# Global attention on one core: value products issued four key blocks at a time, score maxima from the full 128-row operand, and one product that places a chunk's maxima

## The chip, the cores and the metric

One core of a Trainium2 chip runs the whole program. The metric is device time in microseconds (us); the kernel before takes 3729.62 us, the median of 3 runs (3728.04 to 3729.76).

## What is computed

The reference is a one-layer encoder trunk over 2,048 + 256 tokens. Four mixers (neighbourhood attention, a state-space scan, global attention, a gated recurrence) share one input projection; their normalized outputs go through one output product, then come cross-attention to a memory and a convolutional gated feed-forward part. The change touches the global attention alone:

```
def attend_block(qi):
    s = jnp.einsum('bqhgd,bkhd->bhgqk', qi, k).astype(jnp.float32) * scale
    p = jax.nn.softmax(s, axis=-1).astype(v.dtype)
    return jnp.einsum('bhgqk,bkhd->bqhgd', p, v)
```

There are 4 query heads and 2 key/value heads of 64 features, so two query heads share a key head. The 2,048 sample tokens attend to each other, and the 256 prompt tokens to each other.

## The kernel before, in words

`stage_gqa` is a generator. For each of the two key heads (kv) it goes through five chunks of queries: four of 512 queries against 2,048 keys, and one of 256 queries against 256 keys. Keys stand in blocks of 128.

**Operands.** A float32 number is kept as a high and a low part. `ks` holds the high part of the keys twice, in rows 0 to 63 and in rows 64 to 127. For each query head `qs` holds the high part of the queries in the upper 64 rows and the low part in the lower 64, and `qa` the high part and, in its lower 64 rows, minus the maximum of each query. `ka` has the low part of the keys, zeros, and a row of ones against that maximum. So a score block `ps` is two products of 512 columns (L1470, L1471), over all 128 rows, and has its maximum subtracted already.

**Maxima (`gqa_prep`, L1413).** For 128 queries and 512 keys two products `pm`, one for each head, give scores from high parts only (L1429). They take 64 rows each: head 0 the upper half of the array, head 1 the lower, from an operand `qm` with both heads above one another. VectorE reduces each to a maximum (L1432, L1438). Then for each head four products on 64 columns (L1447) write the maxima of four query blocks in rows, and ScalarE copies them negated into `qa` (L1449). `pm` and `pb` share two PSUM buffers. `gqa_prep` yields after each pair of `pm`, and the scores of the chunk before call it: `prep_step()` after each second score, and after the first too in every third key block. So the maxima of a chunk are found during the scores of the chunk before it; those of each kv's first chunk come ahead of its scores.

**Scores (`GqaUnit.scores`, L1463).** After the two products ScalarE takes the exponential into `pe` (L1473). `ps` has two PSUM buffers. GpSimd adds `pe` to the running sum of the chunk, or VectorE for head 0 in odd key blocks (L1481).

**Values (`GqaUnit.values`, L1485).** For one key block two products of plain float32 (L1498), one for each head, go to the upper and the lower 64 columns of the array. Each appears in the trace as two records. They are called when more than AHEAD = 2 key blocks are in flight, so after every key block.

**Order.** TensorE's and SyncE's instructions stand in the order in which Python issues them; the other engines' order is set by the scheduler. `weave` runs `stage_gqa` against a filler, in turn the rest of the input projection, the gate of the state-space mixer (L1244, L1258), neighbourhood attention (L547, L567, L580) and products with the memory (L1588). Each number that `stage_gqa` yields is owed to the filler, and each filler step pays some of it off: FILL = 260 after each score and ahead of each block's values, so 780 for a key block.

Of the kernel before, what the change touches and what calls it, by code (L numbers as in the profile page):

```python
# [13 lines left out]
F32 = mybir.dt.float32  # L14
F32R = mybir.dt.float32r
I32 = mybir.dt.int32
U32 = mybir.dt.uint32
AF = mybir.ActivationFunctionType
ALU = mybir.AluOpType
AX = mybir.AxisListType  # L20
# [3 lines left out]
P = 128  # L24
# [23 lines left out]
UP, DN = slice(0, 64), slice(64, 128)  # L48


def f32(ap):
    return ap.bitcast(F32)
# [91 lines left out]
def drain(g):  # L144
    for _ in g:
        pass
# [1144 lines left out]
def stage_gqa(k, ctx, side=None):  # L1291

    nc, tc = k.nc, k.tc
    pp = ctx.enter_context(tc.tile_pool(name="gq_p", bufs=1, side=side, reuse_waits="tile"))
    wp = ctx.enter_context(tc.tile_pool(name="gq_w", bufs=2, side=side, reuse_waits="tile"))
    sm = ctx.enter_context(tc.tile_pool(name="gq_s", bufs=2, side=side, reuse_waits="tile"))
    ps_m = ctx.enter_context(tc.tile_pool(name="gq_pm", bufs=GQ_M, space=PSUM, side=side))
    ps_s = ctx.enter_context(tc.tile_pool(name="gq_ps", bufs=GQ_S, space=PSUM, side=side))
    ps_o = ctx.enter_context(tc.tile_pool(name="gq_po", bufs=1, space=PSUM, side=side))
    pools = (pp, wp, sm, ps_m, ps_s, ps_o)  # L1300
    chunks = [(c, 512, 0, T_S) for c in range(0, T_S, 512)] + [(T_S, T_P, T_S, T_P)]

    def steps():
        keys = gqa_tiles(k, pp)
        todo = [(kv, ch) for kv in range(2) for ch in chunks]
        loaded = []

        def fetch():
            if todo:
                loaded.append(gqa_queries(k, *todo.pop(0), wp))  # L1310

        for kv in range(2):
            gqa_keys(k, kv, keys)
            if not loaded:
                fetch()
            yield GQ_START
            preps = itertools.chain.from_iterable(gqa_prep(k, keys, ch, loaded, fetch, pools) for ch in chunks)
            ready = []

            def prep_step():  # L1320
                if not ready:
                    x = next(preps, None)
                    if x:
                        ready.append(x)

            flight, late = [], []

            def values():
                u = flight.pop(0)
                u.values()  # L1330
                if late:
                    if next(late[0], late) is late:
                        late.pop(0)
                if u.done:
                    late.append(u.finish())

            for ch in chunks:
                while not ready:
                    prep_step()
                    yield GQ_PREP  # L1340
                unit = GqaUnit(k, kv, keys, ch, ready.pop(0), pools)
                for kb in range(unit.nkb):
                    for h in range(2):
                        unit.scores(kb, h)
                        if h or kb % 3 == 2:
                            prep_step()
                        yield FILL
                    flight.append(unit)
                    if len(flight) > AHEAD:
                        yield FILL  # L1350
                        values()
            while flight:
                yield FILL_END
                values()
            for g in late:
                drain(g)
                yield FILL_END

    return steps()


FILL = 260
FILL_END = 1000
GQ_START = 6000
GQ_PREP = 800
AHEAD = 2
GQ_M = 2
GQ_S = 2
RPM = 3
# [1 line left out]

def gqa_tiles(k, pp):

    nc = k.nc
    ks = pp.tile([P, T], F32R, name="gq_ks")
    ka = pp.tile([P, T], F32R, name="gq_ka")
    va = pp.tile([P, NB, 64], F32, name="gq_va")
    nc.gpsimd.memset(f32(ka)[DN, :], 0.0)
    nc.gpsimd.memset(f32(ka)[64:65, :], 1.0)
    one = pp.tile([P, 1], F32, name="gq_one")  # L1380
    nc.vector.memset(one, 1.0)
    return ks, ka, va, one


def gqa_keys(k, kv, keys):
    nc, s = k.nc, k.s
    ks, ka, va = keys[:3]
    hs = slice(64 * kv, 64 * kv + 64)
    for rows, src, dst in ((UP, "kh", ks), (DN, "kh", ks), (UP, "kl", ka)):
        nc.sync.dma_start(out=f32(dst)[rows, :], in_=s[src][0, hs, :])  # L1390
    nc.sync.dma_start(out=va, in_=s["vc"][:, hs].rearrange("(b p) c -> p b c", p=P))


def gqa_queries(k, kv, chunk, wp):


    nc, s = k.nc, k.s
    q0, nq = chunk[:2]
    qsl = slice(q0, q0 + nq)
    qm = wp.tile([P, 512], F32R, tag="qm", name="qm", bufs=2)  # L1400
    nc.sync.dma_start(out=f32(qm)[:, :nq], in_=s["qh"][kv, :, qsl])
    out = []
    for h in range(2):
        qs = wp.tile([P, 512], F32R, tag=f"qs{h}", name="qs", bufs=3)
        qa = wp.tile([P, 512], F32R, tag=f"qa{h}", name="qa", bufs=3)
        hs = slice(64 * h, 64 * h + 64)
        for rows, src, dst in ((UP, "qh", qs), (DN, "ql", qs), (UP, "qh", qa)):
            nc.sync.dma_start(out=f32(dst)[rows, :nq], in_=s[src][kv, hs, qsl])
        out.append((qs, qa))
    return qm, out  # L1410


def gqa_prep(k, keys, chunk, loaded, fetch, pools):  # L1413


    nc = k.nc
    pp, wp, sm, ps_m, ps_s, ps_o = pools
    q0, nq, k0, nk = chunk
    ks = keys[0]
    nqb = nq // P  # L1420
    half = min(512, nk)
    qm, out = loaded.pop(0)
    fetch()
    mxs = [sm.tile([P, 4, 4], F32, tag=f"mx{h}", name="mx") for h in range(2)]
    for qb in range(nqb):
        for i, kc in enumerate(range(k0, k0 + nk, half)):
            pms = [ps_m.tile([P, 512], F32, tag="m", name="pm") for h in range(2)]
            for hs, pm in zip((UP, DN), pms):
                nc.tensor.matmul(pm[:, :half], lhsT=qm[hs, qb * P:qb * P + P], rhs=ks[hs, kc:kc + half],  # L1429
                                 start=True, stop=True)  # L1430
            for mx, pm in zip(mxs, pms):
                nc.vector.tensor_reduce(out=mx[:, qb, i:i + 1], in_=pm[:, :half], axis=AX.X, op=ALU.max)  # L1432
            yield None
    ms = []
    for h, mx in enumerate(mxs):
        if nk > half:
            m1 = sm.tile([P, 4], F32, tag=f"m1{h}", name="m1")
            nc.vector.tensor_reduce(out=m1[:, :nqb], in_=mx[:, :nqb], axis=AX.X, op=ALU.max)  # L1438
        else:
            m1 = mx[:, :, 0]  # L1440
        ms.append(m1)
    yield None
    for m1, (qs, qa) in zip(ms, out):
        yield None
        pb = ps_m.tile([P, 4, P], F32, tag="m", name="pb")
        for qb in range(nqb):
            nc.tensor.matmul(pb[DN, qb, :], lhsT=m1[:, qb:qb + 1].to_broadcast([P, 64]), rhs=k.ident,  # L1447
                             start=True, stop=True)
        nc.scalar.activation(out=qa[DN, :nq], in_=pb.rearrange("p a b -> p (a b)")[DN, :nq], func=AF.Copy,  # L1449
                             scale=-1.0)  # L1450
    yield out


class GqaUnit:
# [8 lines left out]
    def scores(self, kb, h):  # L1463
        k, nc, nq = self.k, self.k.nc, self.nq
        pp, wp, sm, ps_m, ps_s, ps_o = self.pools
        ks, ka = self.keys[:2]
        qs, qa = self.prep[h]
        ksl = slice(self.k0 + kb * P, self.k0 + kb * P + P)
        ps = ps_s.tile([P, 512], F32, tag="s", name="ps")
        nc.tensor.matmul(ps[:, :nq], lhsT=ks[:, ksl], rhs=qs[:, :nq], start=True, stop=False)  # L1470
        nc.tensor.matmul(ps[:, :nq], lhsT=ka[:, ksl], rhs=qa[:, :nq], start=False, stop=True)  # L1471
        pe = wp.tile([P, 512], F32, tag="pe", name="pe", bufs=2 * AHEAD + 6)
        nc.scalar.activation(out=pe[:, :nq], in_=ps[:, :nq], func=AF.Exp)  # L1473
        eng = nc.vector if h == 0 and kb % 2 else nc.gpsimd
        if kb == 0:
            self.sums[h] = pe
        else:
            t = self.sums[h]
            if kb == 1:
                t = wp.tile([P, 512], F32, tag=f"sum{h}", name="sum")  # L1480
            eng.tensor_tensor(out=t[:, :nq], in0=self.sums[h][:, :nq], in1=pe[:, :nq], op=ALU.add)  # L1481
            self.sums[h] = t
        self.ahead.append(pe)
# [752 lines left out]
```

## Time and profile before

| what | value |
|---|---|
| median of 3 runs | 3729.62 us |
| the profiled execution's own time | 3726.75 us |
| its span on the core | 3724.7 us |
| mean granted TensorE clock | 0.981 |
| TensorE busy (matmul) in the span | 96% |
| VectorE, ScalarE, GpSimd busy | 49%, 34%, 35% |
| first `pm`, last global attention product | at 923.2 us and about 1521 us |

The page gives busy shares of the whole span, the chain of work that ended last and the costliest groups by source line. Views of one stretch (busy time by window, groups by line in a window, who waited for whom, instructions in order of time) tell more of a stage. In the view in order of time the first number is the start, the second the time that a group of equal instructions was busy. Matmuls overlap their neighbours, so the step from one start to the next, not the busy time, is what an instruction takes of TensorE.

### The profile page before, as it was taken

Reading aid. Unit: us, or ns where it says so; the run is one execution under the profiler, and the core shown is the slowest. Engines: PE = TensorE matmul, PEld = TensorE weight load, DVE = VectorE, ACT = ScalarE, POOL = GpSimd, SP = SyncE. Lnnn points to the kernel's source line nnn. Section 1 sums busy time; section 2 is a strip of 40 time slices with the busy share of each in tenths; the row PEclk is TensorE's granted clock in tenths of the full one; section 3 lists DMA queues with packets and bytes.
Section 4 is the critical chain, followed back from the end, with each engine's and each line's share of the span. In section 5 each row is a group of like instructions: output and inputs, shape, how many; then the busy total and the mean of one; then the engine's idle time right before and its main releaser. Section 6 shows DMA issues by size and latency. Waiting matters only on the chain.

```text
span 3724.7 us, 53214 instructions
## 1 busy us (share of the span) xinstructions
PE 3581.3 (96%) x20150; PEld 3084.8 (83%) x20150; DVE 1822.1 (49%) x4422; ACT 1275.4 (34%) x2632; POOL 1301.0 (35%) x1110
## 2 busy tenths in 40 slices
PE   7998999999899999999998999999999999999998
PEld 6998998898445555678887999988999998999997
DVE  5757777565653644355555333326333336333334
ACT  3321114453345445444444222224322224322222
POOL 3326435343345244200001433433423333433342
PEclk9999999999799999999998999999999999999999
DMA  6453443333141411312224212214211223211221
GB/s 209 165 190 110 164 151 105 108 125 83 44 122 45 118 38 27 129 52 75 74 74 154 74 52 68 74 62 134 87 52 57 68 75 101 87 57 52 63 80 51
DMA packets 212833, 340.37 MB, mean 91 GB/s; under 512 B 82913, under 2 KB 155105, under 8 KB 208353
## 3 DMA queue, kind: packets, MB, share of 16 engines
q1 hardware_dynamic: 212576, 336.97, 28.6%
q8 instruction: 159, 2.61, 0.3%
q14 instruction: 98, 0.79, 0.1%
HBM read 252.14 MB, written 84.77 MB: 90 GB/s over the span
## 4 chain that ended last, share of the span: by engine, by line
PE 83%; DVE 8%; DMA 3%; issue 2%; ACT 2%; POOL 1%; SPq 0%; ACTq 0%; DVEq 0%; POOLq 0%
PE pg L123 5%; PE pa L123 5%; PE pa L124 5%; PE pa L125 5%; PE pg L124 5%; PE pg L125 5%; PE pd L123 5%; PE pd L125 5%; PE pd L124 5%; PE po L1498 4%; PE mm L123 3%; PE mm L125 3%; PE mm L124 3%; PE ps L123 2%; PE pa L691 2%; PE ps L124 2%
## 5 line engine op out<-in xcount | busy, mean ns | idle before, releaser
L1968 DVE SCALAR_TENSOR_TENSOR gc<-pg,f_cw,gc 128x384 f32<-128x384 f32 (+4 forms) x308 | 166.5, 558 | 563.2 <-ACT gc L1958 559.4
L117 POOL TENSOR_TENSOR ul<-raw,uh 128x1024 fp32r<-128x1024 f32 x132 | 317.6, 2406 | 209.3 <-ACT uh L116 206.3
L123 PE MATMUL pg<-h,uh 128*128 128x386 f32 x1056 | 358.7, 340 | 0.9 <-DVE x L1809 0.9
L124 PE MATMUL pg<-h,uh 128*128 128x386 f32 x1056 | 357.6, 339 | 0.0
L125 PE MATMUL pg<-h,ul 128*128 128x386 f32 x1056 | 357.0, 338 | 0.0
L123 PE MATMUL pa<-h,uh 128*128 128x384 f32 x1056 | 356.9, 338 | 0.0
L124 PE MATMUL pa<-h,uh 128*128 128x384 f32 x1056 | 356.5, 338 | 0.0
L125 PE MATMUL pa<-h,ul 128*128 128x384 f32 x1056 | 356.3, 337 | 0.0
L1994 DVE TENSOR_TENSOR acc<-acc,pd 128x512 f32<-128x512 f32 x264 | 181.4, 687 | 312.9 <-PE pd L125 312.8
L123 PE MATMUL pd<-dh,uh 128*128 128x512 f32 x792 | 316.4, 399 | 8.1 <-DVE h L166 5.5
L1976 POOL TENSOR_TENSOR ul<-gc,uh 128x384 fp32r<-128x384 f32 x132 | 134.8, 1021 | 541.1 <-ACT uh L1975 541.1
L125 PE MATMUL pd<-dh,ul 128*128 128x512 f32 x792 | 313.8, 396 | 0.0
L124 PE MATMUL pd<-dl,uh 128*128 128x512 f32 x792 | 313.7, 396 | 0.0
L1481 POOL TENSOR_TENSOR sum<-sum,pe 128x512 f32<-128x512 f32 x168 | 214.2, 1284 | 194.6 <-ACT pe L1473 188.5
L117 POOL TENSOR_TENSOR dl<-raw,dh 128x1024 fp32r<-128x1024 f32 x66 | 158.8, 2406 | 265.1 <-ACT dh L116 265.1
L1958 ACT ACTIVATE gc<-pg,f_cw 128x384 f32<-128x384 f32 x132 | 87.2, 661 | 419.0 <-PE pg L125 415.8
L123 PE MATMUL mm<-wh,hhi 128*128 128x256 f32 x720 | 212.7, 295 | 4.6 <-DVE ut L363 4.0
L1473 ACT ACTIVATE pe<-ps 128x512 f32<-128x512 f32 (+1 forms) x264 | 151.0, 590 | 188.2 <-PE ps L1471 185.5
L123 PE MATMUL mm<-hhi,wh 128*128 128x384 f32 x576 | 208.0, 361 | 0.0
L1432 DVE TENSOR_REDUCE mx<-pm 128x1 f32<-128x512 f32 (+1 forms) x264 | 170.7, 678 | 72.0 <-PE pm L1429 70.9
L124 PE MATMUL mm<-wl,hhi 128*128 128x256 f32 x720 | 205.0, 285 | 0.0
L125 PE MATMUL mm<-wh,hlo 128*128 128x256 f32 x720 | 204.8, 284 | 0.0
(491 smaller groups left out, 8704.2 us busy)
## 6 DMA issues: line engine op xcount, KB each, us to landing
raw<-in_w_up SPq DMA_DIRECT2D x132, 512.0 KB
raw<-in_w_down SPq DMA_DIRECT2D x66, 512.0 KB
x<-in_x SPq DMA_DIRECT2D x36, 512.0 KB
hhi<-s_h SPq DMA_DIRECT2D x8, 1536.0 KB
hlo<-s_h SPq DMA_DIRECT2D x8, 1536.0 KB
raw<-in_w_in SPq DMA_DIRECT2D x22, 512.0 KB
s_h<-hhi SPq DMA_DIRECT2D x6, 1536.0 KB
s_h<-hlo SPq DMA_DIRECT2D x6, 1536.0 KB
```

Source lines behind the costliest of these rows:

```text
L117: (eng or nc.gpsimd).tensor_tensor(out=l, in0=raw, in1=f32(h), op=ALU.subtract)
L123: mm(out, lhsT=lh, rhs=rh, start=first, stop=False)
L124: mm(out, lhsT=lh, rhs=rl, start=False, stop=False)
L125: mm(out, lhsT=ll, rhs=rh, start=False, stop=last)
L1432: nc.vector.tensor_reduce(out=mx[:, qb, i:i + 1], in_=pm[:, :half], axis=AX.X, op=ALU.max)
L1473: nc.scalar.activation(out=pe[:, :nq], in_=ps[:, :nq], func=AF.Exp)
L1481: eng.tensor_tensor(out=t[:, :nq], in0=self.sums[h][:, :nq], in1=pe[:, :nq], op=ALU.add)
L1498: nc.tensor.matmul(po[hs, :nq], lhsT=va[:, vt, :], rhs=pe[:, :nq], start=kb == 0, stop=self.done)
L1958: nc.scalar.activation(out=gc, in_=pg[:, 1:TG + 1], func=AF.Identity, scale=cw[:, f, 1:2], bias=cw[:, f, 3:4])
L1968: V.scalar_tensor_tensor(out=gc[:, a:b], in0=pg[:, a + off:b + off], scalar=cw[:, f, tap:tap + 1], in1=gc[:, a:b], op0=ALU.mult, op1=ALU.add)
L1976: nc.gpsimd.tensor_tensor(out=ul[:, cs], in0=gc, in1=f32(uh)[:, cs], op=ALU.subtract)
L1994: V.tensor_tensor(out=acc[b][:, ns], in0=acc[b][:, ns], in1=pd, op=ALU.add)
```

## The change

Three things change. **Values** are issued for four key blocks at once, when six are in flight (AHEAD + BATCH); ahead of them there is no yield any more, and FILL is 340, so a key block now owes 680 to the filler. `pe` gets 13 buffers in place of 10. **Maxima** come from `qs` and `ks` over all 128 rows, so `qm` and its load go, and both products of a pair use the whole array. **Placing:** the maxima of a chunk are reduced into columns 64 to 67 of a 128x128 tile of zeros (two sets of two tiles), one product with the identity turns it, and VectorE multiplies its lower half, spread over the query blocks, by a small matrix `place` with -1 on its diagonal. Each query's row then has its maximum in one of four rows of `qa`, and `ka` has ones in these four.

```
             def values(n):
                 for _ in range(n):
                     u = flight.pop(0)
                     u.values()
                     if u.done:
                         late.append(u.finish())
                 for _ in range(2):
                     if late and next(late[0], late) is late:
                         late.pop(0)
...
                     flight.append(unit)
-                    if len(flight) > AHEAD:
-                        yield FILL
-                        values()
-            while flight:
-                yield FILL_END
-                values()
+                    if len(flight) == AHEAD + BATCH:
+                        values(BATCH)
+            yield FILL_END
+            values(len(flight))
...
-FILL = 260
-FILL_END = 1000
+FILL = 340
+FILL_END = 3000
 AHEAD = 2
+BATCH = 4
...
-    nc.gpsimd.memset(f32(ka)[64:65, :], 1.0)
+    nc.gpsimd.memset(f32(ka)[64:68, :], 1.0)
+    mzs = [[pp.tile([P, P], F32, name=f"gq_mz{i}{h}") for h in range(2)] for i in range(2)]
...
+    nc.vector.tensor_scalar(out=place[DN], in0=k.ident[DN, 64:68], scalar1=-1.0, scalar2=None, op0=ALU.mult)
...
-    qm = wp.tile([P, 512], F32R, tag="qm", name="qm", bufs=2)
-    nc.sync.dma_start(out=f32(qm)[:, :nq], in_=s["qh"][kv, :, qsl])
...
-            for hs, pm in zip((UP, DN), pms):
-                nc.tensor.matmul(pm[:, :half], lhsT=qm[hs, qb * P:qb * P + P], rhs=ks[hs, kc:kc + half],
+            for (qs, qa), pm in zip(out, pms):
+                nc.tensor.matmul(pm[:, :half], lhsT=qs[:, qb * P:qb * P + P], rhs=ks[:, kc:kc + half],
...
-        for qb in range(nqb):
-            nc.tensor.matmul(pb[DN, qb, :], lhsT=m1[:, qb:qb + 1].to_broadcast([P, 64]), rhs=k.ident,
-                             start=True, stop=True)
-        nc.scalar.activation(out=qa[DN, :nq], in_=pb.rearrange("p a b -> p (a b)")[DN, :nq], func=AF.Copy,
-                             scale=-1.0)
+        pb = ps_m.tile([P, P], F32, tag="m", name="pb")
+        nc.tensor.matmul(pb, lhsT=mz, rhs=k.ident, start=True, stop=True)
+        nc.vector.tensor_tensor(out=qa[DN, :nq].rearrange("p (b q) -> p b q", q=P),
+                                in0=pb[DN].unsqueeze(1).to_broadcast([64, nqb, P]),
+                                in1=place[DN, :nqb].unsqueeze(2).to_broadcast([64, nqb, P]), op=ALU.mult)
...
-        pe = wp.tile([P, 512], F32, tag="pe", name="pe", bufs=2 * AHEAD + 6)
+        pe = wp.tile([P, 512], F32, tag="pe", name="pe", bufs=2 * (AHEAD + BATCH) + 1)
```

The order of TensorE's instructions in the first chunk, before (`ps` scores or, on L1244, the filler's gate; `pm` maxima; `po` values):

```order
L1498 MATMUL po<-pe,gq_va 64x512 x2
L1470 MATMUL ps<-qs,gq_ks 128x512
L1471 MATMUL ps<-qa,gq_ka 128x512
L1244 MATMUL ps<-y_10162,gw 128x288
L1244 MATMUL ps<-y_10163,gw 128x288
L1244 MATMUL ps<-y_10162,gw 128x288
L1244 MATMUL ps<-y_10163,gw 128x288
L1470 MATMUL ps<-qs,gq_ks 128x512
L1471 MATMUL ps<-qa,gq_ka 128x512
L1429 MATMUL pm<-gq_ks,qm 128x512 x2
L1498 MATMUL po<-pe,gq_va 64x512 x2
```

And of the change, at the end of that chunk's scores (L1471 and L1472 are now the scores, L1499 the values, L1448 the product that places the maxima):

```order
L1244 MATMUL ps<-y_10168,gw 128x288
L1244 MATMUL ps<-y_10169,gw 128x288
L1244 MATMUL ps<-y_10168,gw 128x288
L1244 MATMUL ps<-y_10169,gw 128x288
L1471 MATMUL ps<-qs,gq_ks 128x512
L1472 MATMUL ps<-qa,gq_ka 128x512
L1499 MATMUL po<-pe,gq_va 64x512 x8
L1471 MATMUL ps<-qs,gq_ks 128x512
L1472 MATMUL ps<-qa,gq_ka 128x512
L1448 MATMUL pb<-ident,gq_mz_9930 128x128
L1471 MATMUL ps<-qs,gq_ks 128x512
L1472 MATMUL ps<-qa,gq_ka 128x512
```

Where one pair of value products followed each key block, eight now stand together. In the whole program there are 131 separate groups of value products before and 34 in the change, 72 products of maxima to rows before and 20 now; the 264 `pm`, 264 scores and 264 value products are all still there.

VectorE's order in the change, where the first chunk's maxima are placed (L1439 the reductions of `pm`, L1443 those into the tile of zeros, L1449 the multiplication into `qa`; L1233 to L1237 are the filler's):

```order
L1439 TENSOR_REDUCE mx<-pm 128x1 x2
L1237 SCALAR_TENSOR_TENSOR y_10168<-t,y_10168 128x576
L1233 TENSOR_SCALAR t<-t 128x576
L1443 TENSOR_REDUCE gq_mz_9928<-mx 128x4
L1443 TENSOR_REDUCE gq_mz_9929<-mx 128x4
L1235 TENSOR_TENSOR t<-t,y_10169 128x576
L1233 TENSOR_SCALAR t<-t 128x576
L1449 TENSOR_TENSOR qa<-pb,gq_place 64x512
L1237 SCALAR_TENSOR_TENSOR y_10169<-t,y_10169 128x576
L1449 TENSOR_TENSOR qa<-pb,gq_place 64x512
```

The write into `qa` has moved from ScalarE to VectorE, and stands there behind the filler's work.

## Rows read from the trace of the kernel before

**Rows 1.** The page: span, and busy time by engine.

```profile
span 3724.7 us, 53214 instructions
PE 3581.3 (96%) x20150; PEld 3084.8 (83%) x20150; DVE 1822.1 (49%) x4422; ACT 1275.4 (34%) x2632; POOL 1301.0 (35%) x1110
```

**Rows 2.** Busy us (instructions) by engine, granted clock, DMA share, GB/s, by window.

```profile
core 0: us, PE busy (x) PEld busy (x) DVE busy (x) ACT busy (x) POOL busy (x), PEclk, DMA share, GB/s
923.00:958.40 35.40, 28.77 (x114) 17.56 (x113) 28.28 (x48) 5.93 (x9) 4.64 (x3) 0.74 0.51 159
958.40:1046.50 88.10, 80.24 (x277) 37.02 (x276) 48.87 (x78) 39.99 (x69) 39.23 (x40) 0.87 0.06 19
1046.50:1106.70 60.20, 57.05 (x243) 27.74 (x241) 34.32 (x62) 29.46 (x54) 33.39 (x37) 1.00 0.41 133
1169.30:1212.20 42.90, 42.90 (x222) 24.77 (x220) 11.71 (x39) 24.40 (x59) 23.00 (x21) 1.00 0.17 45
```

**Rows 3.** TensorE in order of time, first chunk: start, us busy, instruction.

```profile
974.01 1.97 PE L1498 MATMUL po<-pe,gq_va 128*64 128x512 f32 x4
975.91 0.80 PE L1470 MATMUL ps<-qs,gq_ks 128*128 128x512 f32 x1
976.50 0.63 PE L1471 MATMUL ps<-qa,gq_ka 128*128 128x512 f32 x1
976.93 0.63 PE L1470 MATMUL ps<-qs,gq_ks 128*128 128x512 f32 x1
...
979.79 0.40 PE L1470 MATMUL ps<-qs,gq_ks 128*128 128x512 f32 x1
980.02 0.40 PE L1471 MATMUL ps<-qa,gq_ka 128*128 128x512 f32 x1
...
995.35 0.39 PE L1471 MATMUL ps<-qa,gq_ka 128*128 128x512 f32 x1
995.66 0.49 PE L1429 MATMUL pm<-gq_ks,qm 64*128 64x512 f32 x2
996.09 1.08 PE L1498 MATMUL po<-pe,gq_va 128*64 128x512 f32 x4
997.10 0.50 PE L1470 MATMUL ps<-qs,gq_ks 128*128 128x512 f32 x1
997.43 0.40 PE L1471 MATMUL ps<-qa,gq_ka 128*128 128x512 f32 x1
```

**Rows 4.** TensorE in order of time, the end of the second kv.

```profile
1515.49 1.08 PE L1498 MATMUL po<-pe,gq_va 128*64 128x256 f32 x8
1516.50 0.66 PE L1512 MATMUL pt<-ident,ou 128*128 128x128 f32 x4
```

**Rows 5.** TensorE in order of time, a placing of maxima.

```profile
1163.07 0.40 PE L1471 MATMUL ps<-qa,gq_ka 128*128 128x512 f32 x1
1163.39 0.65 PE L1447 MATMUL pb<-ident,mx 128*64 128x128 f32 x4
1163.98 0.55 PE L567 MATMUL pt<-ident,na_pe 128*128 128x128 f32 x3
```

**Rows 6.** VectorE's groups by line, 1046.5 to 1106.7 us: busy, mean ns, idle before.

```profile
L1432 DVE TENSOR_REDUCE mx<-pm 128x1 f32<-128x512 f32 x33 | 21.6, 685 | 7.9 <-PE pm L1429 7.7
L1481 DVE TENSOR_TENSOR sum<-sum,pe 128x512 f32<-128x512 f32 x7 | 4.8, 689 | 14.7 <-ACT pe L1473 14.7
```

**Rows 7.** ScalarE's exponentials, groups by line, 1169.3 to 1212.2 us.

```profile
L1473 ACT ACTIVATE pe<-ps 128x512 f32<-128x512 f32 (+1 forms) x26 | 13.9, 564 | 13.0 <-PE ps L1471 12.3 <-POOL sum L1481 0.6
```

**Rows 8.** TensorE's waits (us, times, longest), 1046.5 to 1106.7, then 958.4 to 974 us.

```profile
PE pm L1429 <- DVE mx L1432: 2.8, 4, 1.2
...
PE pm L1429 <- DVE mx L1432: 3.3, 2, 2.4
PE ps L1470 <- ACT pe L1473: 2.6, 2, 1.4
```

**Rows 9.** ScalarE's copies into `qa`: ns min/median/max, first and last start.

```profile
L1449 ACT ACTIVATE qa<-pb x20: 379/593/594, 956.8 to 1473.1; 64x512 fp32r<-64x512 f32 x16, 64x256 fp32r<-64x256 f32 x4
```

More of the change, by code (lines that the diff above doesn't have):

```diff
@@ L1326, in steps, with values @@
             flight, late = [], []
[L1328 to L1332, printed above, removed]
+            def values(n):
+                for _ in range(n):
+                    u = flight.pop(0)
+                    u.values()
+                    if u.done:
+                        late.append(u.finish())
+                for _ in range(2):
+                    if late and next(late[0], late) is late:
                         late.pop(0)
-                if u.done:
-                    late.append(u.finish())
             for ch in chunks:
@@ L1378, in gqa_tiles @@
     nc.gpsimd.memset(f32(ka)[DN, :], 0.0)
-    nc.gpsimd.memset(f32(ka)[64:65, :], 1.0)
+    nc.gpsimd.memset(f32(ka)[64:68, :], 1.0)
     one = pp.tile([P, 1], F32, name="gq_one")
     nc.vector.memset(one, 1.0)
-    return ks, ka, va, one
+    mzs = [[pp.tile([P, P], F32, name=f"gq_mz{i}{h}") for h in range(2)] for i in range(2)]
+    for mz in mzs:
+        for m in mz:
+            nc.gpsimd.memset(m, 0.0)
+    place = pp.tile([P, 4], F32, name="gq_place")
+    nc.vector.tensor_scalar(out=place[DN], in0=k.ident[DN, 64:68], scalar1=-1.0, scalar2=None, op0=ALU.mult)
+    return ks, ka, va, one, mzs, place
 def gqa_keys(k, kv, keys):
@@ L1409, in gqa_queries @@
         out.append((qs, qa))
-    return qm, out
+    return out
 def gqa_prep(k, keys, chunk, loaded, fetch, pools):
@@ L1418, in gqa_prep @@
     q0, nq, k0, nk = chunk
-    ks = keys[0]
+    ks, place = keys[0], keys[5]
     nqb = nq // P
     half = min(512, nk)
-    qm, out = loaded.pop(0)
+    out = loaded.pop(0)
     fetch()
+    mzs = keys[4][0]
+    keys[4].append(keys[4].pop(0))
     mxs = [sm.tile([P, 4, 4], F32, tag=f"mx{h}", name="mx") for h in range(2)]
@@ L1427, in gqa_prep @@
             pms = [ps_m.tile([P, 512], F32, tag="m", name="pm") for h in range(2)]
-            for hs, pm in zip((UP, DN), pms):
-                nc.tensor.matmul(pm[:, :half], lhsT=qm[hs, qb * P:qb * P + P], rhs=ks[hs, kc:kc + half],
+            for (qs, qa), pm in zip(out, pms):
+                nc.tensor.matmul(pm[:, :half], lhsT=qs[:, qb * P:qb * P + P], rhs=ks[:, kc:kc + half],
                                  start=True, stop=True)
-            for mx, pm in zip(mxs, pms):
-                nc.vector.tensor_reduce(out=mx[:, qb, i:i + 1], in_=pm[:, :half], axis=AX.X, op=ALU.max)
+            for mx, mz, pm in zip(mxs, mzs, pms):
+                to = mx[:, qb, i:i + 1] if nk > half else mz[:, 64 + qb:65 + qb]
+                nc.vector.tensor_reduce(out=to, in_=pm[:, :half], axis=AX.X, op=ALU.max)
             yield None
[L1434 to L1441, printed above, removed]
+    if nk > half:
+        for mx, mz in zip(mxs, mzs):
+            nc.vector.tensor_reduce(out=mz[:, 64:64 + nqb], in_=mx[:, :nqb], axis=AX.X, op=ALU.max)
     yield None
-    for m1, (qs, qa) in zip(ms, out):
+    for mz, (qs, qa) in zip(mzs, out):
         yield None
-        pb = ps_m.tile([P, 4, P], F32, tag="m", name="pb")
-        for qb in range(nqb):
-            nc.tensor.matmul(pb[DN, qb, :], lhsT=m1[:, qb:qb + 1].to_broadcast([P, 64]), rhs=k.ident,
-                             start=True, stop=True)
-        nc.scalar.activation(out=qa[DN, :nq], in_=pb.rearrange("p a b -> p (a b)")[DN, :nq], func=AF.Copy,
-                             scale=-1.0)
+        pb = ps_m.tile([P, P], F32, tag="m", name="pb")
[3 more added lines that the diff above has]
+                                in1=place[DN, :nqb].unsqueeze(2).to_broadcast([64, nqb, P]), op=ALU.mult)
     yield out
```

## The prediction

> **What bounds the kernel now.** I read the page first, then busy time by window, then TensorE in order of time, and last the groups and waits of single stretches. The page says that TensorE is busy for 96% of the span and no other engine for half of it [rows 1]. A busy share can hide waits, so the windows come next. In the global attention they show two regimes. In the first 35 us VectorE is busy 28.3 of 35.4 us and the granted clock is 0.74 [rows 2]: reductions of maxima pace TensorE there. From 1046.5 us on TensorE is busy for 57.1 of 60.2 us, or all of 42.9, at a granted clock of 1.00 [rows 2]. TensorE is the bound in these chunks, and time taken from it is time gained, as long as nothing takes its place.
>
> What TensorE's time goes into is seen from start to start. Inside a row of scores a product takes 0.23 us (979.79 to 980.02) [rows 3]. Around other shapes there is more: 0.31 from a score to the maxima (995.35 to 995.66), 0.33 for the first score after values (997.10 to 997.43) [rows 3], 0.32 from a score to the placing products [rows 5]. Each change between whole-array, half-row and half-column products costs about 0.1 on either side. This is what the change removes.
>
> **Values, 131 groups to 34 runs.** A group alone takes 1.01 (996.09 to 997.10); at the low clock level, 1.2 in place of 2.4 GHz, it took 1.90 (974.01 to 975.91) [rows 3]. If only the columns double, columns are 0.89 and the fixed part is 0.12. With 0.09 to get in and 0.10 to get out, a group alone pays 0.31. That a run pays this once is shown by the one place where two groups already stand together: eight records of 256 columns take 1.01 (1515.49 to 1516.50) [rows 4], as much as four of 512. So 97 x 0.31 = 30 us less.
>
> **Maxima on all rows.** A pair now takes 0.43 (995.66 to 996.09) [rows 3], with 0.08 in and 0.10 out: 0.61. On all rows the two follow each other, and I price each as a score product of the same columns, 0.23: 0.46 a pair, 0.15 less. 29 pairs stand right ahead of values and share the way out; they save 0.05, and 0.09 of the sum above must be given back for them. Of 132 pairs, 33 stand ahead of a kv's first scores, where TensorE isn't the bound, and count nothing. (99 - 29) x 0.15 - 29 x 0.04 = 9 us less. The rows show first that the half-row pair pays 0.18 for its neighbours and saves 0.23 by running side by side, with 0.20 more until the next may start. Against this, the Trainium skill (TensorEngine Tiling (Array Packing), When to Use Tiling) says that a contraction of 64 calls for two-fold row tiling, which is just what the change gives up. By that rule a pair goes from 0.23 to 0.46 and this term is 99 x 0.23 = 23 us more, not 9 less; it is the fourth rival below.
>
> **Placing.** Four records take 0.59 (1163.39 to 1163.98) after 0.09 to get in [rows 5]; at 0.11 a record, eight take 1.03. Now one product of two records, 0.22, stands in a row of whole-array products. 16 placings of eight records save 0.90, 4 of four save 0.46: 16 us less.
>
> The three together: **55 us** of TensorE.
>
> **What is late next.** Before, values came after each key block, and during their 1.01 us VectorE and ScalarE caught up. Now scores of four key blocks stand together, then values alone for about 4 x 0.89 + 0.31 = 3.9 us. Only two `pm` and two `ps` buffers exist, so the others can take little of their backlog into the run of values.
>
> Take four key blocks with maxima. TensorE: 16 score products, 3.7; 5 1/3 pairs at 0.46, 2.5; filler, 4 x 680, some 2.7 if the program's unit is a nanosecond. Together 8.9. VectorE: 10 2/3 reductions at 0.65 (21.6 us for 33), 7.0; two sums at 0.69, 1.4 [rows 6]; the rest of its 34.3 us [rows 2], a quarter of about 7, 1.7. Together 10.1. So VectorE is 1.2 us behind in each such run. The lower end is 0: one pair of maxima, 1.3 us, is reduced under the values. The upper end is 2.4: each of the two sums holds VectorE's queue, the reductions behind it included, until its exponential is there, 0.6 (VectorE stood 14.7 us at such sums in a chunk [rows 6]). I take 1.1. The 99 pairs fill 18 or 19 runs: 18 x 1.1 = 20 us, 0 to 43.
>
> The other 16 runs have no maxima. TensorE needs 3.7 + 2.7 = 6.4, ScalarE eight exponentials of 0.6, 4.8, and (24.4 - 13.9) / 13 x 4 = 3.2 of other work [rows 2, 7]: 8.0. Some of that runs under values; 0 to 1.5 us a run, and I take 0.4: 6 us, 0 to 24.
>
> **What costs nothing.** The negated write into `qa` goes from ScalarE, 0.59 [rows 9], to VectorE, 0.69 by its sums [rows 6], 20 times; three scores stand on TensorE between a placing and the first score that needs it, 1.4 us, and without that cover it would be 0.7 each, 14 us. GpSimd's four memsets and one small VectorE operation come once, beside the projection. One load in seven goes from SyncE's queue of queries; the first `pm` now waits for the second head's low part in place of `qm`, and projection products cover it. A key block owes 100 less to the filler, 13 us in all: that is TensorE's work wherever it stands, and the order shows ten more rows of memory products behind the stage. The first kv's early part stays with VectorE.
>
> **The sum.** 55 - 26 = 29 us less: 3726.75 - 29 = 3698 us. The profiled execution is 2.9 us under the median of the runs; I keep 3698. About 0.2% (7.5 us) is what a measurement of this kernel can tell from no change.
>
> **The rivals.**
> 1. *Forecast*, 0.70: waits give back 17 to 45 of the 55 us, 3678 to 3716.
> 2. *VectorE and ScalarE become the bound*, 0.09: both near their upper ends, 46 to 65 us given back, 3717 to 3737. For it: between 958.4 and 974 us, where the kernel before has scores and maxima without values, TensorE waits 5.9 us in 15.6 [rows 8]. Against it: the filler's gate work stood on VectorE there; in the next chunk it waits for maxima for 2.8 us in 60 [rows 8].
> 3. *The runs of values absorb it all*, 0.09: 8 to 16 us given back, or none, 3671 to 3679. For it: VectorE is busy 34 of 60 us [rows 2].
> 4. *Half-row pairs were as cheap as the skill's rule has them*, 0.06: the maxima cost 23 us more, so 30 + 16 - 23 - 26 = 3 us slower, 3730. Against it: 0.43 from a pair to its successor.
> 5. *Slower: the clock falls in the runs of scores*, 0.06. Place: the scores and maxima of the 18 runs, where TensorE stops for VectorE again and again. At the low level a product takes 0.43 (976.50 to 976.93) [rows 3], 0.20 more. The 29 us are gone once 145 products run there, and the result is slower by more than 0.2% from 183 of the 792; with half of the 480 in those runs, 240 x 0.20 = 48 us, 3746. For it: the clock was 0.87 in the first chunk, with such waits. Against it: 1.00 in the second, with waits of up to 1.2 us [rows 2, 8].
>
> **The numbers.** The range 3675 to 3722 takes in the forecast, about half of the second rival and half of the third, 0.8 together. Faster by over 0.2% means below 3722: 0.70 + 0.09 + 0.05 = 0.84. Within 0.2%: the rest of the second rival and the fourth, 0.10. Slower: the fifth, 0.06.
>
> **What would show it.** Right: eight value products with starts in all within 3.6 to 3.8 us to the next score; `pm` starts 0.23 apart and no longer 0.43 to the next instruction; a placing of 0.22; and TensorE's waits for maxima in the second chunk grown from 2.8 us to about 5 to 8. Wrong: waits for maxima and exponentials of over 45 us in the stage, value records further apart inside a run than in a single group, or a granted clock under 0.9 in the chunks after the first.

## The result, and the profile after

The change takes 3680.61 us (median of 4 runs, 3678.42 to 3683.75) against 3729.69 for the kernel before, measured beside it: a ratio of 0.9867, with a 95% interval of 0.9853 to 0.988, 49 us faster. The forecast was 3698, so the change is 17 us faster than forecast, inside the range. A second measurement (e11, below) gave 0.9869.

The profiled execution took 3678.42 us at a mean granted clock of 0.984. The page of the change, span and busy time by engine:

```profile
span 3676.5 us, 52998 instructions
PE 3513.9 (96%) x20046; PEld 3094.6 (84%) x20046; DVE 1852.2 (50%) x4443; ACT 1257.9 (34%) x2612; POOL 1313.5 (36%) x1114
```

Against [rows 1] TensorE's busy time fell by 67 us while its share stayed at 96%, and VectorE's rose by 30 us. The whole gain lies in the global attention: from the first `pm` to the last product with the memory, which is the filler's end, the kernel before takes 628.9 us (923.15 to 1552.0) and the change 581.0 (921.0 to 1502.0). The rest of the span is about 3096 us in both.

Busy time by window of the change, at the same places as [rows 2]: the first `pm`, the first score, the ends of chunks (us, then busy time and instructions of PE, PEld, DVE, ACT, POOL, granted clock, DMA share, GB/s):

```profile
921.00:952.70 31.70, 23.28 (x102) 15.27 (x100) 27.84 (x48) 5.54 (x9) 3.25 (x2) 0.79 0.54 166
952.70:1038.30 85.60, 74.58 (x278) 41.75 (x278) 58.82 (x88) 38.35 (x68) 43.89 (x43) 0.92 0.05 16
1038.30:1097.50 59.20, 53.93 (x231) 31.77 (x229) 36.41 (x60) 28.07 (x52) 32.09 (x35) 0.94 0.37 127
1148.70:1187.10 38.40, 38.14 (x212) 24.49 (x210) 13.30 (x35) 22.78 (x56) 22.87 (x19) 1.00 0.17 46
```

The first chunk, from its first score to the end of its values, went from 88.1 to 85.6 us and its granted clock from 0.87 to 0.92. The second hardly got shorter (60.2 to 59.2): TensorE is busy for 3 us less there, but no longer nearly all the time, and the clock went from 1.00 to 0.94. The stretch without maxima went from 42.9 to 38.4 with TensorE still full. A chunk of 16 key blocks also owes the filler 1,600 less (1.6 us, if the unit is a nanosecond), and that work comes behind the scores. So where TensorE was the bound with nobody near it, most of the time taken from it came through; where VectorE stood close behind, much of it was given back.

TensorE of the change in order of time, from the second and third chunk's scores (start, us busy, instruction, idle before it):

```profile
1045.72 1.10 PE L1435 MATMUL pm<-gq_ks,qs 128*128 128x512 f32 x2 [1.05 <-DVE mx L1439]
...
1051.43 3.65 PE L1499 MATMUL po<-pe,gq_va 128*64 128x512 f32 x16
1055.01 0.50 PE L1471 MATMUL ps<-qs,gq_ks 128*128 128x512 f32 x1
...
1060.23 1.09 PE L1435 MATMUL pm<-gq_ks,qs 128*128 128x512 f32 x2 [1.45 <-DVE mx L1439]
...
1071.43 0.38 PE L1448 MATMUL pb<-ident,gq_mz 128*128 128x128 f32 x2
1071.57 0.48 PE L1471 MATMUL ps<-qs,gq_ks 128*128 128x512 f32 x1
1071.88 0.39 PE L1472 MATMUL ps<-qa,gq_ka 128*128 128x512 f32 x1
...
1075.39 0.39 PE L1472 MATMUL ps<-qa,gq_ka 128*128 128x512 f32 x1
1075.63 0.63 PE L1435 MATMUL pm<-gq_ks,qs 128*128 128x512 f32 x2
1076.09 0.39 PE L1471 MATMUL ps<-qs,gq_ks 128*128 128x512 f32 x1
1076.32 0.39 PE L1472 MATMUL ps<-qa,gq_ka 128*128 128x512 f32 x1
```

Eight value products take 3.58 us to the next score (1051.43 to 1055.01), where four separate pairs took 1.01 each with 0.2 around them [rows 3]. A pair of maxima that waits for nothing takes 0.46 to its successor (1075.63 to 1076.09), as much as two scores, with 0.24 and 0.23 on either side, in place of 0.43 and its surroundings. A pair at 1045.72 was busy for 1.10 us after an idle 1.05: there it waited for VectorE's reductions. A placing takes 0.14, and the score behind it 0.08 more than usual: the 0.22 of the forecast.

### The profile page after: what moved, and what is told of

The parts are those of the page before. It is cut to its first block, busy times and chain, and to the rows that moved or that the text cites. A ratio compares the mean times of both kernels' runs of the same rounds, so it can differ in the third digit from the quotient of the medians.

```text
span 3676.5 us, 52998 instructions
## 1 busy us (share of the span) xinstructions
PE 3513.9 (96%) x20046; PEld 3094.6 (84%) x20046; DVE 1852.2 (50%) x4443; ACT 1257.9 (34%) x2612; POOL 1313.5 (36%) x1114
## 4 chain that ended last, share of the span: by engine, by line
PE 55%; DVE 3%; DMA 1%; ACT 1%; issue 0%; SPq 0%; ACTq 0%; DVEq 0%
PE pg L123 5%; PE pa L123 5%; PE pa L124 5%; PE pa L125 5%; PE pg L124 5%; PE pg L125 5%; PE pd L123 5%; PE pd L124 5%; PE pd L125 5%; PE ps L123 2%; PE ps L125 2%; PE ps L124 2%; DMA mx<-s_mix 1%; PE po L1778 1%; PE tr L164 1%; PE pt L1765 0%
## 5 line engine op out<-in xcount | busy, mean ns | idle before, releaser
L123 PEld LDWEIGHTS pg<-h,uh 128*128 128x128 f32 x1056 | 198.8, 188 | 2.1 <-issue 1.3
```

What stands on the lines that cost most here:

```text
L123: mm(out, lhsT=lh, rhs=rh, start=first, stop=False)
```

## The experiments

**One part at a time.** Four kernels side by side, the kernel before at 3729.09 us. e1 takes the values in runs alone, e2 the maxima on all rows alone, e3 the placing alone, and e4 the last two together, with values after each key block.

The edit of e1, against the kernel before:

```
-                    if len(flight) > AHEAD:
-                        yield FILL
-                        values()
+                    if len(flight) == AHEAD + BATCH:
+                        values(BATCH)
...
-FILL = 260
+FILL = 340
...
-        pe = wp.tile([P, 512], F32, tag="pe", name="pe", bufs=2 * AHEAD + 6)
+        pe = wp.tile([P, 512], F32, tag="pe", name="pe", bufs=2 * (AHEAD + BATCH))
```

> The runs of four key blocks alone: the order of values and the filler's share as in the change, maxima and their placing as before; exponentials have 12 buffers, not 13, since the load of the maxima's own operand stays in memory. Theory A (the forecast's sum, each term as written): 30 us less on TensorE, 26 us of new waits, so 3722 to 3728. Theory B (the new waits are small, since VectorE catches up under the runs): 30 us less and 5 to 12 of waits, 3704 to 3711. Theory C (the gain beyond the forecast is TensorE's clock in the first chunk, and comes with the maxima on all rows): waits as in A, and the first chunk's granted clock stays near 0.87.

e1: 3708.7 us, ratio 0.995 (0.9931 to 0.9969), 20 us faster, inside theory B's range.

The edit of e2 (`qm` and its load go):

```
-            for hs, pm in zip((UP, DN), pms):
-                nc.tensor.matmul(pm[:, :half], lhsT=qm[hs, qb * P:qb * P + P], rhs=ks[hs, kc:kc + half],
+            for (qs, qa), pm in zip(out, pms):
+                nc.tensor.matmul(pm[:, :half], lhsT=qs[:, qb * P:qb * P + P], rhs=ks[:, kc:kc + half],
```

> Maxima on all rows alone. Theory A: 9 us less, 3718 to 3723, clock of the first chunk as before. Theory of the tiling rule: a pair costs 0.23 more, 23 us more, 3750. Theory C: 9 us less and 8 to 12 more from the clock, whose granted value in the first chunk goes from 0.87 to about 0.94: 3708 to 3713.

e2: 3703.58 us, ratio 0.9928 (0.9914 to 0.9943), 25 us faster, more than any of the three theories allowed.

The edit of e3:

```
-            nc.tensor.matmul(pb[DN, qb, :], lhsT=m1[:, qb:qb + 1].to_broadcast([P, 64]), rhs=k.ident,
-                             start=True, stop=True)
-        nc.scalar.activation(out=qa[DN, :nq], in_=pb.rearrange("p a b -> p (a b)")[DN, :nq], func=AF.Copy,
-                             scale=-1.0)
+        nc.tensor.matmul(pb, lhsT=mz, rhs=k.ident, start=True, stop=True)
+        nc.vector.tensor_tensor(out=qa[DN, :nq].rearrange("p (b q) -> p b q", q=P),
```

> The placing by one product alone. Theory A: 16 us less on TensorE, 3711 to 3716. Rival: the multiplication stands in VectorE's queue and the first score of a chunk waits for it, 20 times 0.7, so 14 of the 16 are given back: 3726 to 3730.

e3: 3707.12 us, ratio 0.9943 (0.9927 to 0.9959), 22 us faster, somewhat more than theory A's.

The edit of e4, against the change:

```
-                    if len(flight) == AHEAD + BATCH:
-                        values(BATCH)
+                    if len(flight) > AHEAD:
+                        yield FILL
+                        values()
...
-FILL = 340
+FILL = 260
```

> The change without the runs of values: maxima on all rows and the placing, values after every key block. Theory A: 25 us less than before, 3702 to 3707, and the runs of values are then worth 22 to 27 of the change's 49. Theory C: 35 less, 3692 to 3697, with the clock of the first chunk near 0.94. If the three parts are independent, the differences of this run and of the runs of values alone add up to the change's 49 us.

e4: 3684.81 us, ratio 0.9881 (0.9864 to 0.9897), 44 us faster, again more than either theory.

What follows: the parts alone give 20, 25 and 22 us, 67 in all, and together 49. Maxima and placing add up (25 + 22 = 47 against 44); the runs of values do not. Alone they are worth 20 us, on top of the other two 4 to 5 (0.9881 against 0.9867 and 0.9869, with intervals that overlap; in the traces e4's stage takes 586.8 us and the change's 581.0). What the runs take from TensorE, priced from rows: four groups alone are 4 x 1.01 with 0.19 around each, 4.80; a run is 3.58 + 0.19 = 3.77. Each of the 97 groups that join a run saves 0.34, together 33 us. So about 28 of the 33 were given back.

Where to is seen in who waited for whom, 915 to 1465 us (us, times, longest; PE is the matmul queue, PEld the weight loads). For e4:

```profile
PEld pm L1435 <- DVE mx L1439: 46.4, 78, 3.3
...
PE pm L1435 <- DVE mx L1439: 15.9, 25, 3.0
...
PE ps L1471 <- ACT pe L1474: 0.8, 3, 0.4
```

And for the change:

```profile
PEld pm L1435 <- DVE mx L1439: 66.5, 116, 3.3
...
PE pm L1435 <- DVE mx L1439: 22.1, 31, 3.0
...
PE ps L1471 <- ACT pe L1474: 5.3, 10, 2.0
...
PE ps L1472 <- DVE qa L1449: 1.1, 2, 0.9
```

Waits for maxima grew most, by 6 us on the matmul queue and 20 on the loads, those for exponentials by 4.5. The matmul queue's 10.7 are the part of the 28 that these rows name; TensorE's whole idle time between 920 and 1400 us grew by 13, from 29.0 to 42.3. The rest then lies in busy time that got longer, as in the pair at 1045.72, and wasn't separated further. For the multiplication into `qa` on VectorE TensorE waited 1.1 us in all.

**Rows or clock.** The maxima gave 25 us where their products, priced from rows, give 11. e5 keeps e2's instructions and order, but the pair uses 72 of 128 rows. e9 and e10 repeat e2 and e5 side by side on another chip, and e11 the change.

```
-                nc.tensor.matmul(pm[:, :half], lhsT=qs[:, qb * P:qb * P + P], rhs=ks[:, kc:kc + half],
+                nc.tensor.matmul(pm[:, :half], lhsT=qs[:72, qb * P:qb * P + P], rhs=ks[:72, kc:kc + half],
```

> Maxima alone changed, as in the run of maxima on all rows, but from 72 of the 128 rows: the high parts and 8 of the 64 rows of low parts, the other 56 left out. The columns, the instructions, their order and the whole-array arrangement are those of that run (3703.6 us; stretches at the low clock level in the stage 37.5 us against 68.3 before). Theory R (the rows in use decide the granted clock): the low stretches come back to 55 to 70 us and the time to 3712 to 3718. Theory S (the changes of arrangement, with the array running empty around each, decide it): low stretches of 35 to 45 us and 3700 to 3706 us.

> Maxima on all rows alone once more, now beside the 72-row form on one chip. Theory R (the rows in use decide the granted clock): mean clock over the span 0.002 or more above that of the kernel before and of the 72-row form, and 6 to 10 us faster than the latter. Theory S (the changes of arrangement decide it): the same clock and time as the 72-row form.

> The 72-row form (56 of the 64 rows of low parts left out of the maxima) on the same chip. Theory R: mean clock as in the kernel before, within 0.001, and 15 to 19 us faster than it, from the shorter sequence on TensorE alone. Theory S: 23 to 28 us faster, as on all rows.

The 56 query rows left out of the maxima of e5 and e10 belong to the low parts. e5: 3707.63 us against 3724.9, ratio 0.9956 (0.9939 to 0.9974), 17 us faster. On the other chip, against 3728.66: e9 3704.84, 0.9939 (0.9926 to 0.9951), 24 us; e10 3706.76, 0.9942 (0.9928 to 0.9956), 22 us, between the two theories. Busy time in the first and the later part of the stage (columns as above), for the kernel before:

```profile
920.00:1040.00 120.00, 105.51 (x384) 55.27 (x383) 74.04 (x120) 43.19 (x73) 41.07 (x39) 0.83 0.21 66
1040.00:1400.00 360.00, 349.06 (x1568) 187.42 (x1568) 177.74 (x428) 174.03 (x395) 149.64 (x140) 0.96 0.30 79
```

For e9, all rows:

```profile
920.00:1040.00 120.00, 105.25 (x417) 60.98 (x416) 77.74 (x127) 45.42 (x78) 45.44 (x44) 0.87 0.19 56
1040.00:1400.00 360.00, 345.33 (x1633) 203.89 (x1633) 187.29 (x450) 181.51 (x413) 158.05 (x145) 0.99 0.30 81
```

For e10, 72 rows:

```profile
920.00:1040.00 120.00, 104.96 (x413) 60.87 (x412) 77.56 (x127) 45.64 (x78) 45.23 (x44) 0.87 0.18 55
1040.00:1400.00 360.00, 345.73 (x1608) 206.29 (x1608) 184.36 (x441) 178.32 (x405) 153.93 (x142) 0.96 0.29 78
```

And for the change:

```profile
920.00:1040.00 120.00, 100.56 (x401) 59.71 (x399) 87.22 (x136) 43.88 (x76) 47.14 (x45) 0.89 0.19 57
1040.00:1400.00 360.00, 337.13 (x1643) 212.01 (x1643) 217.50 (x482) 181.34 (x419) 174.15 (x155) 0.99 0.30 81
```

Since a low stretch runs at half speed, the time at the low level is about twice what the clock lacks of 1, times the length: before 2 x 0.17 x 120 + 2 x 0.04 x 360 = 70 us, e9 31 + 7 = 38, e10 31 + 29 = 60, the change 26 + 7, nearly 34. All rows bring the clock up in both parts, 72 rows in the first alone; e2 and e5 show the same (34 and 60 us). The times of e9 and e10 are nearly equal, and their intervals overlap. But in the traces the stage, from the first `pm` to the last product with the memory, takes 605.4 us in e9 and 611.7 in e10 (e2 604.4, e5 609.6, before 628.9). The rest of the span, which none of these edits touches, took 3097.4 us in e9 and 3090.7 in e10 and hides the difference. Part of it is seen where the maxima of the second kv stand ahead of its scores, for the kernel before, e9 and e10 in turn:

```profile
1226.80:1265.40 38.60, 36.43 (x167) 23.37 (x166) 26.96 (x74) 15.93 (x46) 2.14 (x4) 0.87 0.66 158
1216.90:1250.50 33.60, 30.45 (x166) 21.90 (x166) 26.22 (x71) 14.60 (x43) 2.13 (x4) 1.00 0.69 166
1220.80:1257.70 36.90, 32.89 (x165) 24.06 (x166) 26.44 (x71) 15.07 (x45) 2.13 (x4) 0.91 0.69 158
```

So with the same instructions in the same order, and as many changes of arrangement (298 in the stage of both forms, 520 before), the rows in use go with the granted clock and with 5 to 6 us of the stage: side by side in e9 and e10, and on two further chips in e2 and e5. What the fewer changes themselves do to the clock stays open. TensorE's idle time did not shrink in either (14.5 + 10.9 us before, 14.8 + 14.7 in e9, 15.0 + 14.3 in e10), so the 13 or 14 us beyond the products are in no wait. The clock has room for them, by an estimate from these rows: 11 us of products and at most 16 of clock (half of the 32 us of low stretches that went), less 4 of longer idle time, are 23 us, as much as e9's stage lost. How much of the low stretches TensorE was busy in wasn't measured.

> The change itself on the same chip as the runs beside it, 47 to 51 us faster than the kernel before. It is the measure for the run with more filler.

e11: 3679.57 us (3677.78 to 3681.89), ratio 0.9869 (0.9854 to 0.9884): the first result again.

**Is VectorE the pace?** Three kernels beside e5, before at 3724.9 us. e6 is the change with each reduction over 256 of its 512 columns, so it leaves out the maxima over half of the keys:

```
-                nc.vector.tensor_reduce(out=to, in_=pm[:, :half], axis=AX.X, op=ALU.max)
+                nc.vector.tensor_reduce(out=to, in_=pm[:, :half // 2], axis=AX.X, op=ALU.max)
```

> The change, with each reduction of maxima over 256 of its 512 columns: the maximum over the other half of the keys is left out. VectorE's time for a reduction falls by about 0.27 us, 264 times. Theory A (the runs of values put VectorE behind, and its reductions give back some 27 us): 12 to 20 us less than the change, 3660 to 3668. Rival (what is given back is ScalarE's and GpSimd's, or lies in TensorE's own order): under 4 less, 3677 to 3681. Some of the gain will be in the start, where VectorE paces TensorE anyway, up to 5 us.

e6: 3662.91 us, ratio 0.9834 (0.9812 to 0.9856), 62 us faster. Its reductions in the second chunk, by line, 1038 to 1097 us (count, busy us, mean ns, idle before and what ended it):

```profile
L1439 DVE TENSOR_REDUCE mx<-pm 128x1 f32<-128x256 f32 x34 | 13.1, 419 | 13.0 <-PE pm L1435 13.0
```

A reduction took 419 ns in place of 683, and the kernel gained another 12 us on the change (0.9834 against 0.9867, with intervals that just touch), as theory A had it and with TensorE's work untouched. But most of the gain isn't in the runs of scores. The change takes 31.6 us from the first `pm` to the first score (921.03 to 952.65), and from there to the first `pm` of the second kv:

```profile
952.70:1205.40 252.70, 229.37 (x1038) 137.98 (x1037) 146.81 (x279) 123.77 (x258) 129.24 (x122) 0.96 0.23 67
```

In e6 the same two stretches are:

```profile
923.00:944.80 21.80, 18.25 (x102) 14.10 (x101) 14.10 (x40) 1.37 (x2) 0.12 (x1) 0.99 0.53 170
944.80:1198.60 253.80, 228.71 (x1038) 139.50 (x1037) 133.95 (x287) 127.99 (x264) 134.71 (x124) 0.94 0.26 73
```

Ahead of the first scores 9.9 us went, twice what the expectation allowed for the start, and 3.0 ahead of the second kv's; the first kv's scores and values took as long as in the change; from the second kv's first score on 7.6 us went. In all 19 us of this profiled execution's stage went, more than the 12 of the medians. So the length of the reductions sets the pace ahead of the scores and in part of the second kv. What the runs lose in the first kv is not shown to be theirs.

e7 makes the runs half as long (`BATCH = 2`).

> The change with runs of two key blocks (BATCH = 2, 9 buffers for exponentials). The runs go from 34 to about 66, 32 x 0.33 = 11 us more TensorE time. Theory A: VectorE and ScalarE wait shorter between runs, and two thirds of the 27 us given back come home: 7 to 11 us faster than the change, 3670 to 3674. Rival: the waits come from reductions against scores whatever the length of the run: 8 to 11 us slower, 3688 to 3692.

e7: 3679.96 us, ratio 0.988 (0.9864 to 0.9897), in neither theory's range. Its run of values, TensorE in order of time:

```profile
1053.32 1.94 PE L1499 MATMUL po<-pe,gq_va 128*64 128x512 f32 x8
1055.19 0.50 PE L1471 MATMUL ps<-qs,gq_ks 128*128 128x512 f32 x1
```

Two runs of 1.87 us to the next score are 3.74, 0.16 more than one of 3.58, and each has its own 0.19 around it. 32 runs more at 0.35 are 11 us more for TensorE. Its time is 4 to 5 us longer by the ratios, with intervals that overlap widely, and its stage in the trace is 579.8 us against 581.0: most of what the longer runs save is waited away.

e8 owes the filler more after each score, so that more of its work stands between the scores:

```
-FILL = 340
+FILL = 420
```

> The change with FILL = 420 in place of 340: 160 more filler for a key block, so more TensorE work between the maxima. Theory A (VectorE 1.1 us behind in each run with maxima): the waits for maxima in the chunks beside maxima fall by about 0.6 us a run, 10 us in all, and some 3 to 6 are lost where the filler runs out earlier: 3672 to 3678. Rival (the waits are not for want of filler): no change within 3 us, or slower because the last chunk of each kv has less filler: 3679 to 3690.

e8: 3665.02 us, ratio 0.9843 (0.9824 to 0.9863), faster than theory A's range. Repeated beside e11 on another chip:

> The change with FILL = 420 on the same chip. Theory A: 6 to 12 us faster than the change, of which 4 to 7 are waits for maxima that more filler covers, and the rest filler that no longer stands alone behind the stage. Rival: the 10 us seen in the first run of it were the chip's, and the two agree within 3 us.

e12: 3667.11 us (3661.93 to 3668.14), ratio 0.9834 (0.982 to 0.9847), 12.5 us under e11 and 61.5 under the kernel before. This is the fastest complete kernel here. Its busy time in the same windows:

```profile
920.00:1040.00 120.00, 100.43 (x387) 60.62 (x385) 86.69 (x135) 45.61 (x79) 46.93 (x46) 0.87 0.21 64
1040.00:1400.00 360.00, 341.65 (x1722) 217.97 (x1721) 212.46 (x510) 186.84 (x444) 166.93 (x152) 1.00 0.30 80
```

And its waits, 915 to 1465 us:

```profile
PE pm L1435 <- DVE mx L1439: 17.9, 31, 3.0
PE ps L1471 <- ACT pe L1474: 6.2, 12, 1.1
```

From 1040 us on TensorE is busy for 341.7 us in place of 337.1, waits for maxima fell from 22.1 to 17.9, and 79 more of its instructions stand there. These are filler work that came later: in the change the products with the memory start at 1467.6 us and stand alone behind the stage, in e12 the first stand at 1423.9 among the values and scores.

## Why the prediction was right, and where not

**The runs of values: right, 33 us for 30.** A run of four blocks took 3.58 us to the next score, just under the 3.6 to 3.8 that the forecast named, and value records are no further apart in a run than in a group.

**The maxima on all rows: the step that failed.** The term was 9 us; e2 and e9 gave 25 and 24. The products are worth 11, so their pricing held: the pair costs 0.46, as forecast. What the sum lacked is the other 13 or 14, and it had put two things at nothing. One is the clock, which had no term of its own; it came in as the fifth rival alone, which let it fall. It rose, from 0.83 to 0.89 in e2's first 120 us (0.87 in e9) and from 0.96 to 0.99 behind. The other is the 33 pairs (32 in the trace) ahead of a kv's first scores, where TensorE was said not to be the bound. Ahead of the second kv's scores it is busy for 36.4 of 38.6 us in the kernel before, at a clock of 0.87, and e9 takes 33.6 there, at 1.00; ahead of the first kv's it is 35.2 and 33.4. That is 7 of the 23 us that e9's stage lost, clock included. The fourth rival is refuted: at the forecast's price for it e2 would have been 23 us slower, and it was 25 us faster. The Trainium skill (TensorEngine Tiling (Array Packing), When to Use Tiling) calls for two-fold row tiling at a contraction of 64. Here the measurement goes the other way. The Trainium skill (the same page, Key Properties) also says that a change of the tiling mode drains TensorE. The 0.1 us on either side of a half-row pair [rows 3] agree with that, and give it a size.

**Placing: right in kind, somewhat low.** 16 us against 22, with an interval of 15 to 27 (0.9943, 0.9927 to 0.9959).

**What is late next: right in sum, not in its place.** The forecast gave back 26 of the 55 us; e4 and the change show about 28 of the runs' 33. The mechanism named, VectorE behind in the runs of scores, is borne out in kind by the waits for maxima of the stage, 22.1 us in place of 15.9. That the size came out is in part luck. The forecast had reductions as the largest part of VectorE's time, and halving them gave the first kv's scores nothing (e6); it had the sums at 0.69 us, and they took 1.16 on average (last section). It also expected the waits for maxima of the second chunk to grow from 2.8 us to between 5 and 8. They didn't grow; this is the matmul queue's list, 1038.3 to 1097.5 us:

```profile
PE pm L1435 <- DVE mx L1439: 2.5, 2, 1.4
PE ps L1471 <- ACT pe L1474: 2.3, 2, 2.0
```

The loss there stands in stretched pairs and in the lower clock of that window, 0.94.

**The sum.** It added the parts' gains and took off one loss. The three alone add to 67 us and come to 49, 18 less. One reading is that the runs lose more in company of the others: with maxima and placing cheaper, TensorE has less to do in a run of scores, and VectorE is further behind. But e1 alone also lifts the clock, as the maxima do. Its busy time in the windows of e9:

```profile
920.00:1040.00 120.00, 104.46 (x400) 57.57 (x399) 79.39 (x128) 45.90 (x79) 45.12 (x43) 0.87 0.22 68
1040.00:1400.00 360.00, 347.26 (x1632) 198.28 (x1631) 192.07 (x442) 175.94 (x400) 159.26 (x145) 0.98 0.31 81
```

That is 31 + 14 = 46 us at the low level against 70 before, while e4 and the change have 34 alike (0.89 and 0.99). Up to 12 us of e1's gain, half of the difference, is thus a gain that the maxima bring as well and that can't be had twice. How the 18 us divide between the two is open; runs of values with placing and half-row maxima were not tried. The forecast was 17 us too high. The maxima term lacked 15 or 16, the placing 6, the runs 3; against that, 2 us more were given back, maxima and placing together fell 3 short of their sum, and the forecast started from the profiled execution, 3 us under the median. The second and the third rival fell with the 28 us given back, which lie between theirs; the fifth with the clock.

## What to carry to other kernels

Price an operand's shape by the whole stretch from its predecessor to its successor: half-array products that save columns can lose it all to the changes of arrangement around them. When work is taken from the bound engine, compare the second engine's time with it over the same short run of the program, since gains of several such edits need not add once it is close; more independent work from elsewhere in that run (FILL = 420) then recovers time. A forecast on TensorE wants a term for the granted clock, with both signs, wherever the profile shows the clock below 1 in the stretch that changes. And when an edit changes what runs at once, a sum that is split over VectorE and GpSimd wants a price for the two together.

## What was not expected of the hardware

VectorE's sums of exponentials got longer, though nothing in them changed. By line, 1038.3 to 1097.5 us of the change (count, busy us, mean ns, idle before):

```profile
L1439 DVE TENSOR_REDUCE mx<-pm 128x1 f32<-128x512 f32 x32 | 20.6, 683 | 9.6 <-PE pm L1435 9.6
L1482 DVE TENSOR_TENSOR sum<-sum,pe 128x512 f32<-128x512 f32 x7 | 9.4, 1349 | 3.6 <-ACT pe L1474 2.3 <-POOL sum L1482 1.4
```

They take 1349 ns, against 689 in [rows 6], while the reductions beside them, which read `pm`, are as short as before. VectorE in order of time:

```profile
1043.48 1.58 DVE L1482 TENSOR_TENSOR sum<-sum,pe 128x512 f32<-128x512 f32 x1 [0.27 <-ACT pe L1474]
1044.98 2.56 DVE L1439 TENSOR_REDUCE mx<-pm 128x1 f32<-128x512 f32 x4
...
1049.44 0.93 DVE L1482 TENSOR_TENSOR sum<-sum,pe 128x512 f32<-128x512 f32 x1 [0.16 <-ACT pe L1474]
...
1058.02 1.56 DVE L1482 TENSOR_TENSOR sum<-sum,pe 128x512 f32<-128x512 f32 x1 [0.26 <-ACT pe L1474]
```

And GpSimd in the same stretch:

```profile
1041.98 5.44 POOL L1482 TENSOR_TENSOR sum<-sum,pe 128x512 f32<-128x512 f32 x4 [7.14 <-ACT pe L1474]
1048.56 1.27 POOL L1482 TENSOR_TENSOR sum<-sum,pe 128x512 f32<-128x512 f32 x1 [1.14 <-ACT pe L1474]
...
1056.51 2.51 POOL L1482 TENSOR_TENSOR sum<-sum,pe 128x512 f32<-128x512 f32 x2 [3.40 <-ACT pe L1474]
```

Each of these three begins while GpSimd is adding. Over the stage 54 of the change's 64 sums of 512 columns overlap an addition of GpSimd's and average 1.20 us; the other 10 take 0.68 or 0.69. In the kernel before 30 of 64 overlap, and average 0.80. No sum without such an overlap took more than 0.72 in either kernel. Of the change's 44 sums of over 0.70 us, 43 began while GpSimd was adding, and all of these ended 0.55 us after that addition did (for the one at 1049.44, 1050.37 against 1049.83, in rounded numbers). The Trainium skill (SBUF — State Buffer, 🔬 SBUF: two separate sides) says that a VectorE operation with two inputs there and a GpSimd operation that reads there share one pair of ports, and whoever starts first has it to the end. The rows agree: a sum waits for the addition that was there before it. The 56 sums of which each adds to an earlier one cost VectorE 64.8 us in place of 40.6, 24 us that the forecast didn't have, on the engine that TensorE waits for. It comes with the runs of values: the same sums cost 39.8 us in e4, 56.8 in e1 and 54.5 in e12. The pair of maxima at 1045.72 waited behind such a sum: the reductions that freed its buffers began at 1044.98, as the sum of 1043.48 ended. No run took the overlap away, so what this costs the kernel in all is open.
